# Four small edits to a planned whole-model kernel: the table load asked for first, x's sums on GpSimd, forget columns beside the values, the last bank in two halves

## The chip, the core and the metric

One core of one Trainium2 chip. The metric is the device time of one execution in microseconds; lower is better. TensorE (PE) multiplies, ScalarE (ACT) and VectorE (DVE) do the elementwise work and empty PSUM, GpSimd (POOL) helps, SyncE (SP) issues the transfers.

## The reference, cut to what matters

The kernel computes two two-layer blocks one after the other for 256 tokens of width 1024, in fp32. The change touches the first layer (its norm, values and forget gate), and the end (last MLP and final norm).

```python
# first layer, first block
h = rmsnorm(x, norm_gain[layer])            # x * rsqrt(mean(x*x) + EPS) * gain
proj = h @ w_in_ab[j]                       # 1024 -> 4104 columns
qa, ka, va, ga, qb, kb_, vb_, gb, fb = split_cols(proj, AB_SIZES)   # eight of 512, fb of 8
...                                         # moba attention of qa, ka, va; gate ga
log_f = jax.nn.log_sigmoid(fb + b_forget[j])          # used by fox attention of qb, kb_, vb_
yb = from_heads(fox_attention(qb, kb_, vb_, log_f))
...
# end of the second block
h = h + sq_relu_mlp(rmsnorm(h, norm_mlp[i]), mlp_w_in[i], mlp_w_out[i])
return rmsnorm(h, norm_final)
```

## The kernel before

`describe` (L1651) records every operation as an `Op` with its reads and writes. `Plan.schedule` (L264) then runs a list scheduler with a cost for each instruction (`make`, L497) and a priority (longest path to the end, plus a `boost`), decides for operations given with `nc.either` which engine runs them, and writes one order for each engine. `emit` (L453) issues the instructions in that order, so every engine works strictly in the planned order and waits where an input is late. Line 558 issues nearly all instructions, so the profile's rows are told apart by engine, operation and shape, not by line. Since the order is computed from the whole list, an edit to one operation gives a new order everywhere. `PREFER` (L588) makes the planner avoid GpSimd in every choice that has another engine.

Products are made in fp32r from two rounded parts: `split` (L667) gives `hi` (a rounding copy, ScalarE or VectorE) and `lo = raw - hi` (a subtraction of two SBUF tiles, VectorE), and three matmuls add h*wh, h*wl, l*wh in one bank. Weights come in transfers of 512 KB (1024 columns by 128 partitions), cut by `wtiles` (L671) into pieces of up to 512 columns; each piece is split on ScalarE and VectorE. x arrives in four quarters of 128x2x256; `gained` (L914) multiplies it with the norm's gain and splits it too, in eight chunks. The norm's factor r is not in there: it is put onto the results (`scaled`, `qk_scale`), so the projections don't wait for it.

`setup` (L761) issues the constants, then x's quarters and the first weight pieces in turn on SP's queue. Six matmuls of generated numbers (`WARM`) run first on TensorE. `stats_x` (L909) squares x's quarters, adds them, sums over the partitions with a matmul by ones, and takes the power -0.5 on GpSimd (`rsqrt`). It is recorded with `nc.boost = -2e4`, so the planner ranks it behind nearly all else; its squares run on ScalarE, its adds on VectorE.

`layer_ab` (L1155), for the first mixer: projection of q, then k, then `values` (L1067): 512 columns, for each of 2 token tiles and 8 chunks three matmuls with 512 moving columns into a bank of its own; then `forget` (L1108): a transfer of the 8 forget columns, their split, 24 matmuls with 8 stationary columns and 256 moving ones, two small transposes, then log-sigmoid, cumulative sums by matmul, and GpSimd transfers that spread the result over the partitions. It is read by the second mixer alone.

`mlp(1, True)` (L1508) adds the output projection into four banks, `acc[2 * hf + t]`; in the last of 8 groups a boost orders them one after the other. `finish` (L1574) takes each bank as it is ready: sum with the residual, square with an accumulated sum, product with the gain, and after both halves of a token tile the power, the scaling and two transfers out.

Of the kernel before, what the change touches and what calls it, by code (L numbers as in the profile page):

```python
# [14 lines left out]
AF = mybir.ActivationFunctionType  # L15
OP = mybir.AluOpType
# [132 lines left out]
class Op:  # L149
# [4 lines left out]

AHEAD = 4000.0

LAT = {("T", "A"): 196, ("T", "V"): 196, ("T", "G"): 196, ("A", "T"): 271, ("V", "T"): 256, ("G", "T"): 203,
       ("A", "A"): 143, ("V", "V"): 127, ("G", "G"): 102, ("A", "V"): 142, ("V", "A"): 128, ("A", "G"): 170,
       ("G", "A"): 80, ("V", "G"): 155, ("G", "V"): 80}
# [8 lines left out]
class Plan:  # L168
# [95 lines left out]
    def schedule(self):  # L264
        ops = self.ops
        for o in reversed(ops):
            d = min(f[0] for f in o.forms.values())
            e = next(iter(o.forms))
            best = 0.0
            for s, raw in o.succ.items():  # L270
                e2 = next(iter(s.forms))
                best = max(best, s.cp + (lat(e, e2) if raw or e != e2 else 0))
            o.cp = d + best + (2000 if o.kind == "dma_start" else 0)
        for o in ops:
            o.cp += o.boost
        pools = list(self.pools.values())
        for p in pools:
            p.use = np.zeros(len(ops) + 1, int)
# [13 lines left out]
        table = None  # L292
# [28 lines left out]
        n = 0  # L321
        while n < len(ops):
            best = None
            for e in free:
                f, av = fut[e], avail[e]
                while f and (f[0][0] <= free[e] or ops[f[0][2]].done):
                    r, c, i = heapq.heappop(f)
# [4 lines left out]
                t = free[e] if av else (max(free[e], f[0][0]) if f else None)  # L332
# [5 lines left out]
            t, e = best  # L338
# [15 lines left out]
            o = ops[i]  # L354
# [40 lines left out]
            if o.kind == "dma_start":  # L395
                issue = 480 if e == "S" else 1000
                st = max(t + issue, dma_free)
                dma_free = st + d
                free[e] = t + issue
                o.start, o.end = t, st + d + 3000  # L400
            else:
                o.start, o.end = t, t + d
                free[e] = t + d
# [3 lines left out]
            f0 = front  # L407
            while front < len(ops) and ops[front].done:
                front += 1
            woken = set()  # L410
            for b in o.bufs:
                b.left -= 1
                b.free_at = max(b.free_at, o.end + 150)
                if b.left == 0:
                    tg = self.tags[b.tag]
                    p = tg["pool"]
                    p.free.append((b.free_at, b.slot))
                    tg["used"] -= 1
                    p.use[f0:b.last + 1] -= 1
                    woken.add(p)  # L420
            for p in (pools if front > f0 else woken):
                if waiting[p]:
                    wake(p, t)
# [139 lines left out]
S = 256  # L563
# [49 lines left out]

def rows(k0, n, c0, nc_):

    return lambda w: w[k0 * 128:(k0 + n) * 128, c0:c0 + nc_].reshape(n, 128, nc_).transpose(1, 0, 2)


class Net:
# [141 lines left out]
    def setup(self):  # L761
# [115 lines left out]

        return [self.nc.tile([128, 2, 256], "x", "x") for _ in range(4)]

    def stats_sum(self, x):  # L880

        nc = self.nc
        acc = None
        for v in x:
            k = v.shape[1]
            sq = self.t2([128, k, 256], "ssq")
            nc.either(("G", "tensor_tensor", (sq, v, v), {"op": OP.mult}), ("A", "activation", (sq, v, AF.Square), {}))
            if acc is None:
                acc = sq
            else:  # L890
                nc.either(("G", "tensor_tensor", (acc[:, :k], acc[:, :k], sq), {"op": OP.add}),
                          ("V", "tensor_tensor", (acc[:, :k], acc[:, :k], sq), {"op": OP.add}))
        nc.either(("G", "tensor_tensor", (acc[:, 0], acc[:, 0], acc[:, 1]), {"op": OP.add}),
                  ("V", "tensor_tensor", (acc[:, 0], acc[:, 0], acc[:, 1]), {"op": OP.add}))
# [5 lines left out]
    def rms(self, x):  # L900

        nc = self.nc
        v = self.sm([128, NT], "vv")
        nc.vector.tensor_scalar(v, self.stats_sum(x), 1.0 / D, EPS, op0=OP.mult, op1=OP.add)
        r = self.sm([128, NT], "rstd")
        self.rsqrt(r, v)
        return r

    def stats_x(self):  # L909
        self.rstd = self.rms(self.x)  # L910
# [194 lines left out]
        nc.tensor.matmul(o[:, 128:256], v[1][:, sl], pt[:, 256:384], start=False, stop=True, skip_group_check=True)  # L1105


    def forget(self, w, xt):  # L1108

        nc = self.nc  # L1110
        raw = self.t2([128, NC8, 8], "rawf")
        nc.sync.dma_start(raw.rearrange("p c n -> p (c n)"), w.take(64, rows(0, NC8, 4096, 8)))
        fh = nc.tile([128, NC8, 8], "kr", "fh")
        fl = nc.tile([128, NC8, 8], "kr", "fl")
        self.split(raw, fh, fl)
        f = self.sm([128, NT, 8], "f")
        p8 = self.ps("T")[0:8, 0:256]
        for i in range(NC8):
            self.mm_feat(p8, i == 0, xt, fh[:, i], fl[:, i], i, i == NC8 - 1)
        f8 = self.t2([8, 256], "f8")  # L1120
        self.copy(f8, p8)
        pf = self.ps("T")
        for t in range(NT):
            ps = pf[:, t * 8:(t + 1) * 8]
            nc.tensor.transpose(ps, f8[:, t * 128:(t + 1) * 128], self.ident[:8, :8])
        for t in range(NT):
            ps = pf[:, t * 8:(t + 1) * 8]
            nc.vector.scalar_tensor_tensor(f[:, t], ps, self.rstd[:, t:t + 1], self.bfor, op0=OP.mult, op1=OP.add)
# [26 lines left out]
    def layer_ab(self):  # L1155
# [352 lines left out]
    def mlp(self, l, final=False):  # L1508
# [27 lines left out]
        for g in range(G):  # L1536
            hn = hidden(g + 1) if g + 1 < G else None
            if final:
                pieces = [(hf, p) for hf in range(2) for p in self.wtiles(wout, 4 * g, 4, hf * 512, 512)]
                pieces = [(t, *p) for p in pieces for t in range(NT)]  # L1540
                for t, hf, (wh, wl, k, n) in pieces:
                    nc.boost = 0.0 if g < G - 1 else 6e3 - 1.5e3 * (2 * hf + t)
                    self.mm_tok(acc[2 * hf + t], h, wh, wl, n, k - 4 * g, t, k == 0, k + n == FF // 128)
                nc.boost = 0.0
                h = hn
                continue
            for hf in range(2):
# [9 lines left out]
                            self.add_x(acc[bank], bank, rb2)  # L1557
            h = hn
        if final:
            self.finish(xf, acc)  # L1560

    def x_tok(self):

# [7 lines left out]
                self.copy(xf[t][hf], p)  # L1571
        return xf

    def finish(self, xf, acc):  # L1574
# [5 lines left out]
        ss = self.sm([128, NT, 2], "fss")  # L1580
        v = self.sm([128, NT], "fv")
        y = {}
        nc.gate = None
        for hf in range(2):
            for t in range(NT):
                nc.vector.scalar_tensor_tensor(xf[t][hf], acc[2 * hf + t], self.rstd2[:, t:t + 1], xf[t][hf],
                                               op0=OP.mult, op1=OP.add)
                sq = self.t2([128, 512], "fsq")
                nc.scalar.activation(sq, xf[t][hf], AF.Square, accum_out=ss[:, t, hf:hf + 1])
                y[t, hf] = self.t2([128, 512], "fy")  # L1590
                nc.either(*[(e, "tensor_tensor", (y[t, hf], xf[t][hf], gfin[hf]), {"op": OP.mult}) for e in "VG"])
                nc.vector.tensor_scalar(v[:, t:t + 1], ss[:, t, hf:hf + 1], 1.0 / D, EPS if hf == 0 else v[:, t:t + 1],
                                        op0=OP.mult, op1=OP.add)
        for t in range(NT):
            r = self.sm([128, 1], "fr")
            self.rsqrt(r, v[:, t:t + 1])
            for hf in range(2):
                s = slice(hf * 512, (hf + 1) * 512)
                self.scaled(y[t, hf], y[t, hf], r)
                nc.sync.dma_start(self.out[0, t * 128:(t + 1) * 128, s], y[t, hf])  # L1600

    def stick(self):
        nc, a, xt = self.nc, self.a, self.xt
# [135 lines left out]
```

## Time and profile before

| | |
|---|---|
| median of 3 executions | 954.5 us (953.99 to 956.21) |
| the profiled execution | 955.43 us, its span 953.7 us |
| TensorE busy | 937.4 us, 98% |
| VectorE, ScalarE, GpSimd busy | 671.0, 576.7, 56.0 us |
| granted TensorE clock, mean | 0.997 |

The span runs from the first to the last instruction of the profiled execution; the execution's own time is 1.7 us more. A busy TensorE is one with a matmul under way; matmuls overlap, so how fast they follow one another is read from counts in a stretch.

### The profile page before, as it was taken

What the parts mean: (1) busy time and instruction counts of PE and PEld (TensorE: products, weight loads), DVE (VectorE), ACT (ScalarE), POOL (GpSimd) and SP (SyncE); (2) the same over time, 40 slices, a digit from 0 to 9 for tenths busy, and PEclk for the clock granted to TensorE, in tenths of its full rate; (3) what the DMA queues carried; (4) which work ended last, traced back from release to release, by engine and by line L of the source; (5) the groups of instructions that cost most, each with busy time, mean ns of one, the idle gap of its engine ahead of it and who ended that gap; (6) DMA issues with size and microseconds to landing.
All of it is one profiled execution on the core that took longest, in us unless ns stands there. A gap on an engine that the chain in (4) does not pass through costs nothing.

```text
span 953.7 us, 18145 instructions
## 1 busy us (share of the span) xinstructions
PE 937.4 (98%) x6818; PEld 870.0 (91%) x6818; DVE 671.0 (70%) x1544; ACT 576.7 (60%) x1322; POOL 56.0 (6%) x96
## 2 busy tenths in 40 slices
PE   8999999999999999999999999999999999999997
PEld 6787889889989999999999999999899999899985
DVE  7989887686978765995645556856859865555554
ACT  6877666495676684775555545535756755554453
POOL 1061000310301000000000000000000000000000
PEclk9999999999999999999999999999999999999999
DMA  8654436554434443545566566455626465555541
GB/s 289 216 189 156 121 115 190 166 166 140 142 126 132 145 133 125 164 160 177 171 199 182 177 198 200 153 180 177 180 68 218 131 202 178 177 182 194 194 138 44
DMA packets 45369, 157.13 MB, mean 165 GB/s; under 512 B 5464, under 2 KB 5600, under 8 KB 45280
## 3 DMA queue, kind: packets, MB, share of 16 engines
q1 hardware_dynamic: 44928, 154.91, 50.6%
q0 software_dynamic: 352, 1.06, 0.4%
q8 instruction: 53, 0.87, 0.4%
q14 instruction: 36, 0.29, 0.1%
HBM read 154.89 MB, written 1.06 MB: 164 GB/s over the span
## 4 chain that ended last, share of the span: by engine, by line
PE 91%; DVE 4%; ACT 1%; DMA 1%; issue 1%; POOL 1%; POOLq 0%; SPq 0%; DVEq 0%; ACTq 0%
PE psum L558 91%; DVE r L558 2%; DVE k L558 2%; DMA k<-in_w_in_ab_dram 1%; ACT r L558 1%; ACT k L558 1%; POOL k L558 0%; DMA k<-in_x_dram 0%; ACT L558 0%; POOL cd L558 0%; POOLq L1733 0%; SPq L558 0%; DVEq L558 0%; POOLq L558 0%; ACTq L558 0%
## 5 line engine op out<-in xcount | busy, mean ns | idle before, releaser
L558 PE MATMUL psum<-r,r 128*128 128x256 f32 (+1 forms) x6018 | 878.5, 304 | 5.0 <-ACT r L558 2.7
L558 PEld LDWEIGHTS psum<-r,r 128*128 128x128 f32 x6018 | 792.9, 189 | 55.2 <-issue 6.2
L558 DVE TENSOR_TENSOR r<-k,r 128x512 fp32r<-128x512 f32 (+2 forms) x677 | 410.0, 648 | 138.9 <-ACT r L558 67.6
L558 ACT ACTIVATE r<-k 128x512 fp32r<-128x512 f32 (+2 forms) x606 | 327.3, 591 | 149.1 <-PE psum L558 104.8
L558 ACT ACTIVATE k<-psum 128x256 f32<-128x256 f32 (+4 forms) x166 | 69.1, 449 | 144.5 <-PE psum L558 143.0
L558 PE MATMUL psum<-k,k 128*128 128x128 f32 (+8 forms) x748 | 126.1, 304 | 3.5 <-DVE k L558 2.4
L558 PEld LDWEIGHTS psum<-k,k 128*128 128x128 f32 (+3 forms) x748 | 89.0, 166 | 17.7 <-DVE k L558 3.8
L558 POOL TENSOR_TENSOR k<-k,k 128x2 f32<-128x2 f32 (+3 forms) x42 | 48.3, 1163 | 871.1 <-DVE k L558 870.6
L558 ACT ACTIVATE k<-k 128x256 f32<-128x256 f32 (+5 forms) x151 | 72.6, 505 | 16.5 <-DVE k L558 14.3
L558 ACT ACTIVATE k<-k,k 128x256 f32<-128x256 f32 (+2 forms) x144 | 60.7, 446 | 15.4 <-DVE k L558 13.5
L558 DVE TENSOR_TENSOR k<-k 128x256 f32<-128x256 f32 (+3 forms) x36 | 12.5, 352 | 54.3 <-ACT k L558 54.3
L558 DVE TENSOR_TENSOR k<-psum,k 128x512 f32<-128x512 f32 (+2 forms) x61 | 36.8, 608 | 14.4 <-PE psum L558 13.9
L558 DVE TENSOR_TENSOR k<-k,k 128x512 f32<-128x512 f32 (+5 forms) x92 | 44.2, 492 | 1.2 <-POOL k L558 0.9
L558 ACT ACTIVATE r<-k,k 128x256 fp32r<-128x256 f32 x72 | 33.4, 500 | 18.7 <-DVE k L558 17.5
L558 DVE CAST r<-k 128x512 fp32r<-128x512 f32 (+2 forms) x71 | 27.8, 395 | 14.2 <-ACT k L558 9.5
L558 DVE SCALAR_TENSOR_TENSOR r<-k,k,r 128x256 fp32r<-128x256 f32 x80 | 36.0, 478 | 1.0 <-ACT r L558 0.5
L558 DVE TENSOR_TENSOR r<-psum,r 128x256 fp32r<-128x256 f32 (+1 forms) x36 | 17.8, 508 | 13.8 <-ACT r L558 12.7
L558 DVE TENSOR_SCALAR k<-k,k 128x128 f32<-128x128 f32 (+6 forms) x94 | 22.9, 272 | 6.1 <-POOL k L558 5.5
L558 ACT ACTIVATE r<-psum 128x256 fp32r<-128x256 f32 (+1 forms) x34 | 15.2, 460 | 17.6 <-PE psum L558 15.2
L558 DVE CUSTOM_DVE_ANT_0 k<-psum,k 128x256 f32<-128x256 f32 (+1 forms) x48 | 15.6, 350 | 0.5 <-PE psum L558 0.5
L558 DVE TENSOR_REDUCE k<-k 128x8 f32<-128x512 f32 (+2 forms) x21 | 11.4, 571 | 5.3 <-ACT k L558 5.2
L558 ACT ACTIVATION_READ_ACCUMULATOR k<-k,k 128x1 f32 x80 | 15.1, 189 | 0.0
(42 smaller groups left out, 159.6 us busy)
## 6 DMA issues: line engine op xcount, KB each, us to landing
k<-in_mlp_w_in_dram SPq DMA_DIRECT2D x64, 512.0 KB, 4.2
k<-in_mlp_w_out_dram SPq DMA_DIRECT2D x64, 512.0 KB, 4.5
k<-in_w_in_ab_dram SPq DMA_DIRECT2D x32, 512.0 KB, 4.7
k<-in_w_in_cd_dram SPq DMA_DIRECT2D x26, 512.0 KB, 4.0
k<-in_sb_w_qkv_dram SPq DMA_DIRECT2D x24, 512.0 KB, 4.3
k<-in_xa_w_kv_dram SPq DMA_DIRECT2D x16, 512.0 KB, 4.6
k<-in_w_out_ab_dram SPq DMA_DIRECT2D x8, 512.0 KB, 3.7
k<-in_w_out_cd_dram SPq DMA_DIRECT2D x8, 512.0 KB, 3.7
```

The lines of the kernel that those rows point to most:

```text
L558: return getattr(eng, method)(*[real(a) for a in args], **{k: real(v) for k, v in kw.items()})
```

## The change

Four edits, and three that only name things (`LANDING`, `SHAKE`, and `woken`, which keeps its order).

1. `emit` asks for the first activation table that the planned order needs before it issues anything.
2. `stats_x` gets `"G"`: squares and adds of x's statistics have GpSimd as the only engine, and the boost of -2e4 is gone. Other statistics keep the choice.
3. `forget`'s own projection is gone. `values_forget` projects the first mixer's values in two halves: 256 columns for both token tiles into one bank, then 256 columns and the 8 forget columns together, 264 moving columns, into a bank for each token tile.
4. In the last group of the last MLP the bank of the second token tile and second half is summed as 256 columns into its own bank and then 256 into another (`rest`); `finish` adds and squares the halves separately.

```diff
     def emit(self):
-        table = None
+        table = next(o.table[0] for o in self.order if o.eng == "A" and o.table)
+        self.nc.scalar.preload_act_table_set(table)
...
         self.xt = self.gained(self.x, 0)
-        nc.boost = -2e4
-        self.stats_x()
-        nc.boost = 0.0
+        self.stats_x("G")
...
-    def stats_sum(self, x):
+    def stats_sum(self, x, on="GAV"):
...
-            nc.either(("G", "tensor_tensor", (sq, v, v), {"op": OP.mult}), ("A", "activation", (sq, v, AF.Square), {}))
+            calls = (("G", "tensor_tensor", (sq, v, v), {"op": OP.mult}), ("A", "activation", (sq, v, AF.Square), {}))
+            nc.either(*[c for c in calls if c[0] in on])
...
+                nc.either(*[(e, "tensor_tensor", (acc[:, :k], acc[:, :k], sq), {"op": OP.add}) for e in "GV" if e in on])
+        nc.either(*[(e, "tensor_tensor", (acc[:, 0], acc[:, 0], acc[:, 1]), {"op": OP.add}) for e in "GV" if e in on])
...
-    def forget(self, w, xt):
+    def values_forget(self, w, xt):
+        pa = self.acc()
+        for wh, wl, k, n in self.wtiles(w, 0, NC8, 1024, 256):
+            for t in range(NT):
+                s = slice(t * 128, (t + 1) * 128)
+                o = pa[:, t * 256:(t + 1) * 256]
+                for i in range(k, k + n):
...
+        pb = self.proj_tok(w, xt, [*range(1280, 1536), *range(4096, 4104)], 264)
+        v = []
+        for t in range(NT):
+            v.append(self.t2([128, 512], "v"))
+            self.scaled(v[t][:, 0:256], pa[:, t * 256:(t + 1) * 256], self.rstd[:, t:t + 1])
+            self.scaled(v[t][:, 256:512], pb[t][:, 0:256], self.rstd[:, t:t + 1])
+        return v, *self.forget([p[:, 256:264] for p in pb])
+
+    def forget(self, pf):
...
-        for i in range(NC8):
-            self.mm_feat(p8, i == 0, xt, fh[:, i], fl[:, i], i, i == NC8 - 1)
...
-            v = self.values(w, xt, base + 1024)
             if mix == 0:
-                nc.gate = self.late = nc.seen
-                c, ncb = self.forget(w, xt)
-                nc.gate = None
+                self.late = nc.seen
+                v, c, ncb = self.values_forget(w, xt)
+            else:
+                v = self.values(w, xt, base + 1024)
...
+                if g == G - 1:
+                    for wh, wl, k, n, c in end:
+                        nc.boost = 1.0e3 if c == 0 else 0.0
+                        self.mm_tok((rest if c else acc[3])[:, 0:256], h, wh, wl, n, k - 4 * g, 1, c > 0 and k == 4 * g,
+                                    k + n == FF // 128)
...
+                add(t, hf, whole, acc[2 * hf + t])
+                norm(t, hf, hf, low if (t, hf) == (1, 1) else whole)
+        add(1, 1, high, rest[:, 0:256])
+        norm(1, 1, 2, high)
```

## Rows read from the trace of the kernel before

**Rows 1.** The page's first part: busy us (share of the span) and instructions.

```profile
PE 937.4 (98%) x6818; PEld 870.0 (91%) x6818; DVE 671.0 (70%) x1544; ACT 576.7 (60%) x1322; POOL 56.0 (6%) x96
```

**Rows 2.** TensorE's waits over the span: us in total, times, longest us.

```profile
PE psum L558 <- DVE k L558: 2.4, 4, 1.0
PE psum L558 <- DVE r L558: 2.2, 4, 0.9
```

**Rows 3.** Timeline of the start: start us, us, instructions, idle before and its releaser.

```profile
5.34 1.28 ACT L558 ACT_TABLE_LOAD   x1 [5.34 <-DMA k<-in_x_dram]
...
7.97 1.13 ACT L558 ACTIVATE r<-k 128x512 fp32r<-128x512 f32 x2
...
8.63 19.97 PE L558 MATMUL psum<-r,r 128*128 128x512 f32 x80 [2.70 <-ACT r L558]
```

**Rows 4.** TensorE by stretch: length, busy (matmuls), granted clock, DMA share, GB/s.

```profile
10.00:12.00 2.00, 2.00 (x6) 0.54 1.03 414
12.05:28.40 16.35, 16.35 (x73) 1.00 0.92 320
```

**Rows 5.** TensorE's groups, 8.5 to 12.05 us: busy us, mean ns, idle before.

```profile
L558 PE MATMUL psum<-r,r 128*128 128x512 f32 x8 | 3.6, 622 | 2.7 <-ACT r L558 2.7
```

**Rows 6.** DMA issues at 1.65, 2.12 and 2.59 us: size, us to landing.

```profile
k<-in_w_in_ab_dram SPq DMA_DIRECT2D x1, 512.0 KB, 4.9
k<-in_x_dram SPq DMA_DIRECT2D x1, 256.0 KB, 6.4
k<-in_w_in_ab_dram SPq DMA_DIRECT2D x1, 512.0 KB, 7.2
```

**Rows 7.** VectorE's groups by shape, 7.1 to 19.9 us.

```profile
L558 DVE TENSOR_TENSOR r<-k,r 128x512 fp32r<-128x512 f32 x11 | 7.1, 685 | 0.6 <-ACT r L558 0.6
```

**Rows 8.** Timeline of VectorE, 7 to 19 us.

```profile
7.18 0.88 DVE L558 SCALAR_TENSOR_TENSOR r<-k,k,r 128x256 fp32r<-128x256 f32 x2 [0.53 <-ACT r L558]
...
16.41 0.68 DVE L558 TENSOR_TENSOR r<-k,r 128x512 fp32r<-128x512 f32 x1
...
17.62 1.29 DVE L558 TENSOR_TENSOR r<-k,r 128x512 fp32r<-128x512 f32 x2
```

**Rows 9.** VectorE's groups by shape, 251.7 to 255.7 us.

```profile
L558 DVE TENSOR_TENSOR r<-k,r 128x512 fp32r<-128x512 f32 x2 | 2.5, 1232 | 0.0
L558 DVE TENSOR_TENSOR r<-k,r 128x256 fp32r<-128x256 f32 x1 | 1.0, 979 | 0.0
```

**Rows 10.** VectorE's groups by shape, 241.9 to 251 us.

```profile
L558 DVE TENSOR_TENSOR r<-k,r 128x512 fp32r<-128x512 f32 x7 | 4.6, 683 | 0.0
...
L558 DVE TENSOR_TENSOR r<-k,r 128x256 fp32r<-128x256 f32 x2 | 0.8, 418 | 0.0
```

**Rows 11.** GpSimd's adds by shape, 251.6 to 255.7 us, then 256 to 258 us.

```profile
L558 POOL TENSOR_TENSOR k<-k,k 128x256 f32<-128x256 f32 x4 | 3.5, 902 | 0.4 <-PE psum L558 0.4
...
L558 POOL TENSOR_TENSOR k<-k,k 128x256 f32<-128x256 f32 x2 | 1.4, 736 | 0.5 <-DVE k L558 0.5
```

**Rows 12.** Timeline of GpSimd: its first power.

```profile
52.26 1.95 POOL L558 TENSOR_TENSOR k<-k,k 128x2 f32<-128x2 f32 x2 [46.84 <-DVE k L558]
```

**Rows 13.** TensorE's waits, 60 to 110 us.

```profile
PE psum L558 <- DVE k L558: 1.5, 2, 1.0
```

**Rows 14.** Timeline of TensorE among the forget matmuls (128*8).

```profile
30.18 0.40 PE L558 MATMUL psum<-r,kr 128*8 128x256 f32 x2
30.41 0.39 PE L558 MATMUL psum<-r,r 128*128 128x512 f32 x1
30.64 0.39 PE L558 MATMUL psum<-r,kr 128*8 128x256 f32 x2
```

**Rows 15.** TensorE in a stretch of 256-column matmuls.

```profile
420.00:500.00 80.00, 80.00 (x677) 1.00 0.57 181
```

**Rows 16.** Timeline of the tail, VectorE and ScalarE.

```profile
947.11 0.75 DVE L558 SCALAR_TENSOR_TENSOR k<-psum,k,k 128x512 f32<-128x512 f32 x1
947.90 0.63 ACT L558 ACTIVATE k<-k 128x512 f32<-128x512 f32 x1 [0.60 <-DVE k L558]
...
949.53 0.72 ACT L558 ACTIVATE k<-k,k 128x512 f32<-128x512 f32 x1 [0.92 <-POOL k L558]
```

More of the change, by code (lines that the diff above doesn't have):

```diff
@@ L273, in schedule @@
             o.cp = d + best + (2000 if o.kind == "dma_start" else 0)
+        shake = SHAKE * np.random.default_rng(SEED).standard_normal(len(ops))
         for o in ops:
-            o.cp += o.boost
+            o.cp += o.boost + shake[o.i]
         pools = list(self.pools.values())
@@ L399, in schedule @@
                 free[e] = t + issue
-                o.start, o.end = t, st + d + 3000
+                o.start, o.end = t, st + d + LANDING
             else:
@@ L409, in schedule @@
                 front += 1
-            woken = set()
+            woken = {}
             for b in o.bufs:
@@ L419, in schedule @@
                     p.use[f0:b.last + 1] -= 1
-                    woken.add(p)
+                    woken[p] = 0
             for p in (pools if front > f0 else woken):
@@ L1105, in pv_feat @@
         nc.tensor.matmul(o[:, 128:256], v[1][:, sl], pt[:, 256:384], start=False, stop=True, skip_group_check=True)
-    def forget(self, w, xt):
+    def values_forget(self, w, xt):
         nc = self.nc
[L1111 to L1115, printed above, removed]
-        f = self.sm([128, NT, 8], "f")
-        p8 = self.ps("T")[0:8, 0:256]
-        for i in range(NC8):
-            self.mm_feat(p8, i == 0, xt, fh[:, i], fl[:, i], i, i == NC8 - 1)
-        f8 = self.t2([8, 256], "f8")
-        self.copy(f8, p8)
-        pf = self.ps("T")
-        for t in range(NT):
[L1124 to L1128, printed above, removed]
+        pa = self.acc()
[4 more added lines that the diff above has]
+                for i in range(k, k + n):
+                    f = dict(stop=False, skip_group_check=True)
+                    nc.tensor.matmul(o, xt[0][i][:, s], wh[:, i - k], start=i == 0 and t == 0, **f)
+                    nc.tensor.matmul(o, xt[0][i][:, s], wl[:, i - k], start=False, **f)
+                    f["stop"] = i == NC8 - 1
+                    nc.tensor.matmul(o, xt[1][i][:, s], wh[:, i - k], start=False, **f)
+        pb = self.proj_tok(w, xt, [*range(1280, 1536), *range(4096, 4104)], 264)
[5 more added lines that the diff above has]
+        return v, *self.forget([p[:, 256:264] for p in pb])
@@ L1129, in forget @@
+    def forget(self, pf):
+        nc = self.nc
+        f = self.sm([128, NT, 8], "f")
+        for t in range(NT):
+            nc.vector.scalar_tensor_tensor(f[:, t], pf[t], self.rstd[:, t:t + 1], self.bfor, op0=OP.mult, op1=OP.add)
         ab = self.sm([128, NT, 8], "fab")
@@ L1540, in mlp @@
                 pieces = [(t, *p) for p in pieces for t in range(NT)]
+                if g == G - 1:
+                    rest = self.ps("S")
+                    end = [(wh[:, :, c:c + 256], wl[:, :, c:c + 256], k, n, c) for c in (0, 256)
+                           for t, hf, (wh, wl, k, n) in pieces if (t, hf) == (1, 1)]
+                    pieces = [p for p in pieces if p[:2] != (1, 1)]
                 for t, hf, (wh, wl, k, n) in pieces:
@@ L1559, in mlp @@
         if final:
-            self.finish(xf, acc)
+            self.finish(xf, acc, rest)
     def x_tok(self):
@@ L1572, in x_tok, with finish @@
         return xf
-    def finish(self, xf, acc):
+    def finish(self, xf, acc, rest):
         nc = self.nc
@@ L1579, in finish, with add, norm @@
         gfin = [self.bc("gfin", "t2", g[hf], 512) for hf in range(2)]
-        ss = self.sm([128, NT, 2], "fss")
+        nc.gate = None
+        ss = self.sm([128, NT, 3], "fss")
         v = self.sm([128, NT], "fv")
-        y = {}
-        nc.gate = None
+        y = [[self.t2([128, 512], "fy") for _ in range(2)] for _ in range(NT)]
+        def add(t, hf, sl, ps):
+            x = xf[t][hf][:, sl]
+            nc.vector.scalar_tensor_tensor(x, ps, self.rstd2[:, t:t + 1], x, op0=OP.mult, op1=OP.add)
+        def norm(t, hf, c, sl):
+            x = xf[t][hf][:, sl]
+            sq = self.t2([128, 512], "fsq")
+            nc.scalar.activation(sq[:, sl], x, AF.Square, accum_out=ss[:, t, c:c + 1])
+            nc.either(*[(e, "tensor_tensor", (y[t][hf][:, sl], x, gfin[hf][:, sl]), {"op": OP.mult}) for e in "VG"])
+            nc.vector.tensor_scalar(v[:, t:t + 1], ss[:, t, c:c + 1], 1.0 / D, EPS if c == 0 else v[:, t:t + 1],
+                                    op0=OP.mult, op1=OP.add)
+        whole, low, high = slice(0, 512), slice(0, 256), slice(256, 512)
         for hf in range(2):
             for t in range(NT):
[L1586 to L1593, printed above, removed]
+                add(t, hf, whole, acc[2 * hf + t])
+                norm(t, hf, hf, low if (t, hf) == (1, 1) else whole)
+        add(1, 1, high, rest[:, 0:256])
+        norm(1, 1, 2, high)
         for t in range(NT):
```

23 lines of the change are left out of this document (12 added, 11 removed).

## The prediction

> **What bounds the kernel now.** I read the page's engine rows first. TensorE is busy for 937.4 of 953.7 us [rows 1], so the kernel is TensorE work in a row, and only two things can change the time: the work on that engine and its idle time. The view of TensorE's waits comes next: VectorE is waited for eight times, 4.6 us in all [rows 2]. The timeline of the start shows a longer wait, 2.7 us, for ScalarE: its table load begins at 5.34, when the first quarter of x has landed, the first weight piece is rounded at 7.97, and the first real matmul follows at 8.63 [rows 3]. The windows then show a granted clock of 0.54 between 10 and 12 us, behind that gap, mostly the lower of its two levels, 1.2 instead of 2.4 GHz, and 1.00 from 12.05 on [rows 4]. Eight matmuls start from 8.63 to 12.05 [rows 5], 0.427 us each; from 12.05 on, 73 of 512 columns start within 16.35 us, 72 steps of 0.227 [rows 4]. The first projection (48 matmuls) therefore ends at 12.05 + 40 x 0.227 = 21.1 us. The reader is to see that in this first stage TensorE is fed by pairs of instructions on ScalarE and VectorE, and that VectorE works there almost without a pause.
>
> **The table asked for ahead.** The load's 1.28 us leave the path that starts TensorE, unless another stands behind it. The first weight piece is issued at 1.65 and lands 4.9 us later, at 6.55 [rows 6], and its rounding (0.61) would end at 7.25 instead of 8.58. Taken alone: TensorE starts 1.33 us sooner. Its idle gap would then be 1.4 us instead of 2.7; if the clock stayed up, the second weight piece, landing at 2.59 + 7.2 = 9.8 [rows 6], would set the pace: rounded at 10.45, then 36 matmuls, end 18.6, a gain of 2.5. So this stage's lower end is -2.5 us, and -1.3 if the slow stretch only moves. The second load, at 25, delays nothing that TensorE waits for; it counts as nothing.
>
> **x's sums on GpSimd.** Four squarings leave ScalarE, and three adds of 128x512 and a fold leave VectorE, about 0.60 each where they follow one another (0.685 with the overlap [rows 7]; a pair takes 1.29 [rows 8]). GpSimd gets eight two-input instructions in a row: four squarings and three adds of 512 columns, one fold of 256. The trace of before has no 512-wide one. The nearest rows are the 128x256 adds near 252 us: while four of them run, VectorE's two-input instructions take 1.232 us for 512 columns and 0.979 for 256 [rows 9], against 0.683 and 0.418 just before [rows 10]. VectorE is held 0.55 us by each, one of its instructions per GpSimd instruction; GpSimd is held too, 0.902 against 0.736 when VectorE has none of that kind [rows 11]. Doubled for 512 columns (an estimate; the ends are 0.55, if the hold doesn't grow, and 1.47, twice the whole 0.736) that is 1.1 us.
>
> The Trainium skill, "SBUF — State Buffer", section "SBUF: two separate sides", says that a two-input VectorE instruction and a GpSimd instruction exclude each other on a shared port pair for a whole instruction. The rows agree that they exclude each other, but show 0.55 of 0.736 us; by the Trainium skill's rule the sum below would be 2.4 us longer.
>
> The place is the worst one: every piece that TensorE multiplies in this stage needs a 128x256 subtraction of x and a 128x512 one of the weights on VectorE, both two-input [rows 7, 8]. The first squaring (from 5.4 us) falls partly into VectorE's pause of 0.53 before 7.18 [rows 8], and the rest of it is made up by the earlier first rounding. The other seven instructions start when the second quarter of x lands, 2.12 + 6.4 = 8.5 [rows 6], and run back to back with VectorE's: 6 x 1.1 + 0.55 = 7.2 us of holding. Before, the last weight subtraction of the first projection ends at 17.1 [rows 8], behind two of the adds; now at 17.1 - 1.2 + 7.2 = 23.1. The holds end near 19.4, with the fifth of eight pieces due at about 20.4; VectorE then makes a piece in 1.0 us and TensorE needs 6 x 0.227 = 1.36, so TensorE sets the end: 20.4 + 22 x 0.227 = 25.4, against 21.1. I take +4.3 us for the stage, in which the table's gain is lost. Ends: -2.5 (holds that cost nothing) and +6.7 (1.47 each). TensorE starves from about 10 to 20 us, so a half clock there costs little; behind it, it does (a rival).
>
> **What the sums give back.** Before, the statistics were ranked last: GpSimd's first power is at 52.26, after 46.84 us idle [rows 12]. All scaling of q, k and v waits for it, and VectorE then works through it; TensorE waits 1.5 us for it between 60 and 110 us [rows 13]. With the sums done near 20, r is ready some 30 us sooner and this work spreads out; TensorE, itself later, waits less too. Of the 1.5 I take -1.2; ends -1.5 and +1.0, since the planner orders the whole kernel anew and may open a wait of the size of those there are [rows 2]. Late behind it come the weight transfers that wait for VectorE to free their buffers: they slip by up to 6 us, but TensorE reaches those pieces over 5 us later as well, so I add nothing.
>
> **Forget columns in the values.** Removed: 24 matmuls with 8 weight columns. Two of them and one of 512 columns repeat every 0.46 us [rows 14], so each takes (0.46 - 0.227) / 2 = 0.117: 2.8 us; two small transposes, some 0.1 each by the pace of 256 columns. Changed: 48 matmuls of 512 columns become 48 of 256 and 48 of 264. In a stretch of 256-column ones 677, two of them tiny, take 80.0 us, 0.1185 each [rows 15]; 8 columns more are 0.004. So 48 x (0.1185 + 0.1225 - 0.227) = 0.7 us are added. Sum: -3.0 + 0.7 = -2.3 us. TensorE runs without a pause there, so it counts in full; if the 512-column pace is 0.231, it is -2.5, and if weight preparation (eight pieces of 264 columns in place of four of 512) held it up, -1.5. One small DMA and its rounding go, and there is one more accumulator bank for a while. The log-sigmoid chain moves behind the values; its result is needed only by the second mixer, one projection and four pairs of heads later.
>
> **Last bank in two halves.** Before, the tail is: sum 0.75, squaring 0.63 plus the reading of its accumulator, two small steps, the power, scaling 0.72 from 949.53, and the transfer [rows 16]. Now the last sum and square are of 256 columns. By the pair 0.683 and 0.418 [rows 10] the sum saves 0.27; the square saves between nothing and half, I take 0.2; 24 matmuls of 0.1185 in place of 12 of 0.227 add 0.12. Sum -0.35; ends -0.5 and +0.1, the latter if the first half's small steps stand in VectorE's queue ahead of the last sum. Scaling and transfers stay whole. The named landing time (3000 as before), the shake of 0 and the ordered set change nothing.
>
> **Sum.** +4.3 - 1.2 - 2.3 - 0.35 = +0.45 us on the profiled execution's 955.4 us, of which 1.7 lie outside its span. That execution stands 0.9 above the median of 954.5, so against the median I forecast **954.9 us: no change that a measurement can tell** (0.2%, 1.9 us, is about that bound).
>
> **Rivals.** *Faster, 949.5.* The holds hide: VectorE or the transfers had slack there, and the first projection ends between 18.6 and 19.8 us. Then -1.9 - 0.5 - 2.3 - 0.35 = -5.0. For it speaks that before, the last subtraction was done 2.9 us before TensorE needed it; against it, that 7.2 us are more than that. It decides if the holds add less than about 3 us to VectorE's last piece. A milder form, holds of 0.55 each (3.9 instead of 7.2), gives 951.6.
> *Slower, 957.2.* VectorE is held for the whole 0.736 per 256 columns, 1.47 for 512: 6 x 1.47 + 0.74 = 9.6 instead of 7.2, +2.4. This is the rule of the Trainium skill named above. It decides from about 1.35 us per hold. Against it speaks the 0.55 worked out above [rows 9, 10].
> *Slower, 956.5.* The starved stretch lowers the clock as the 2.7 us gap did, and the projection's last eight matmuls run at the slow pace of 0.427: +1.6. One such stretch stands behind a shorter gap [rows 3, 4].
> *The change isn't what it says:* if a load still stood before ScalarE's first copy, 1.28 us would return, but in my main case VectorE covers it; the time stays.
>
> **Chances.** No change 0.40, the faster case with its milder form 0.33, the two slower ones 0.15 and 0.12. So faster 0.33, same 0.40, slower 0.27. The range takes in most of the faster case and both slower ones: 949.5 to 958.0; the main case alone has 954.2 with the low ends of its three small terms together, and 957.1 with the largest high one.
>
> **What would show it.** The table load would stand before 2 us. Behind 8.5 us GpSimd's 512-wide instructions would alternate with VectorE's, whose 512-column subtractions would take about 1.8 us instead of 0.685; TensorE would pause from about 10 us, and its first 48 matmuls would end near 25.4. If they end before 20, the holds were the wrong step. The first power would be at about 20 us, TensorE's wait for VectorE in 60 to 110 us mostly gone, no matmul with 8 weight columns left, and from the last matmul to the end 0.4 us less. I am wrong above all if VectorE keeps its pace under GpSimd's sums, or if the new order opens a wait of more than 2 us later on.

## The result, and the profile after

The changed kernel is slower: 961.7 us median of 6 executions (960.7 to 962.9) against 955.4 of 6 (954.0 to 956.2) of the kernel before; ratio 1.0070, 95% interval 1.0057 to 1.0083. That is above the range that was given (949.5 to 958.0). Its profiled execution has a span of 960.0 us against 953.7, so 6.3 us are to be found.

The page's first part, of the changed kernel:

```profile
PE 940.2 (98%) x6852; PEld 876.4 (91%) x6852; DVE 675.6 (70%) x1546; ACT 583.4 (61%) x1328; POOL 67.3 (7%) x104
```

TensorE's work hardly changed [rows 1]; its waits did (us, times, longest; the view of [rows 2]):

```profile
PE psum L564 <- DVE k L564: 5.7, 4, 2.3
PE psum L564 <- DVE r L564: 3.5, 2, 2.6
```

**The start.** Timeline of the changed kernel, ScalarE, then GpSimd, VectorE and TensorE:

```profile
0.73 1.28 ACT L460 ACT_TABLE_LOAD   x1 [0.73 <-PEq L1753]
...
5.47 1.14 POOL L564 TENSOR_TENSOR k<-k 128x512 f32<-128x512 f32 x1
8.08 3.49 POOL L564 TENSOR_TENSOR k<-k 128x512 f32<-128x512 f32 x2 [1.48 <-DMA k<-in_x_dram]
11.54 1.47 POOL L564 TENSOR_TENSOR k<-k,k 128x512 f32<-128x512 f32 x1
12.96 1.23 POOL L564 TENSOR_TENSOR k<-k 128x512 f32<-128x512 f32 x1
14.14 3.14 POOL L564 TENSOR_TENSOR k<-k,k 128x512 f32<-128x512 f32 x2
17.36 1.06 POOL L564 TENSOR_TENSOR k<-k 128x256 f32<-128x256 f32 x1
...
9.42 5.04 DVE L564 SCALAR_TENSOR_TENSOR r<-k,k,r 128x256 fp32r<-128x256 f32 x4
14.38 3.45 DVE L564 TENSOR_TENSOR r<-k,r 128x512 fp32r<-128x512 f32 x2
17.76 1.34 DVE L564 SCALAR_TENSOR_TENSOR r<-k,k,r 128x256 fp32r<-128x256 f32 x2
...
8.94 4.61 PE L564 MATMUL psum<-r,r 128*128 128x512 f32 x12 [0.81 <-DVE r L564]
16.20 15.04 PE L564 MATMUL psum<-r,r 128*128 128x512 f32 x58 [2.65 <-DVE r L564]
```

The load stands at 0.73 instead of 5.34 [rows 3]. From 8 us on GpSimd's 512-column instructions run back to back with VectorE's: two subtractions that took 1.29 [rows 8] take 3.45, 1.08 us more for each of the two GpSimd instructions beside them; two of 256 columns that took 0.88 take 1.34 beside the fold. TensorE starves at 13.5 and gets its next piece at 16.20. The windows (length, busy, granted clock, DMA share, GB/s; as [rows 4]) show what this does to the clock and to the transfers:

```profile
10.00:12.00 2.00, 2.00 (x6) 0.50 1.03 420
12.00:14.00 2.00, 1.55 (x5) 0.71 1.03 420
14.00:16.00 2.00, 0.00 (x0) 1.00 0.20 80
16.00:18.00 2.00, 1.80 (x5) 0.65 0.00 0
18.00:20.00 2.00, 2.00 (x6) 0.50 0.52 115
20.00:31.00 11.00, 11.00 (x50) 1.00 0.86 301
```

The granted clock is 0.50, wholly the lower level, already between 10 and 12 us, behind waits of 0.80 and 0.81 us at 7.40 and 8.94, and again from 18 to 20 us, behind the long pause. The transfers stop for some 3 us, since VectorE has freed no buffer: between 8 and 20 us SyncE's queue waits for it twice, 10.7 us in all. The 48th matmul of the first projection starts at 25.41, against 20.89 in the trace of before. A second loss stands behind it, in TensorE's timeline: the column sums of x (one moving column), two matmuls, and then a wait for VectorE, which itself waits for GpSimd's power (0.72 us from 31.86):

```profile
31.08 0.50 PE L564 MATMUL psum<-k,k 128*128 128x1 f32 x4
31.44 0.70 PE L564 MATMUL psum<-r,r 128*128 128x512 f32 x2
33.02 0.49 PE L564 MATMUL psum<-k,k 128*128 128x128 f32 x2 [0.88 <-DVE k L564]
33.62 11.72 PE L564 MATMUL psum<-r,r 128*128 128x512 f32 x50
```

At 0.227 each the two matmuls take TensorE to 31.9, the two of 128x128 columns need some 0.2, and the next stands at 33.62: some 1.5 us are lost, an estimate, 0.88 of them in the wait that the profile shows. In e3, described below, twelve matmuls stand there in place of two, and no wait opens.

**Where the rest went.** The column sums of the next norm are landmarks: they end the first layer, and then the second. In the timeline of before they stand here:

```profile
178.34 0.50 PE L558 MATMUL psum<-k,k 128*128 128x1 f32 x4
...
295.54 0.28 PE L558 MATMUL psum<-k,k 128*128 128x1 f32 x2
```

and in the changed kernel here (the line between them is the column sums of the cross-attention's memory, `mem_setup`, which before stood at 49 us, beside x's):

```profile
180.53 0.50 PE L564 MATMUL psum<-k,k 128*128 128x1 f32 x4
...
245.23 0.28 PE L564 MATMUL psum<-k,k 128*128 128x1 f32 x2
...
302.25 0.28 PE L564 MATMUL psum<-k,k 128*128 128x1 f32 x2
```

So: +4.5 us at the 48th matmul, +1.5 at 32 us, back to +2.2 at the end of the first layer (-3.8 on the way), +6.7 at the end of the second (+4.5 in it), +6.3 at the end. The 4.5 us are at the four pairs of sliding-window heads, `layer_cd`'s last part. The timeline of the changed kernel there, TensorE, VectorE, GpSimd:

```profile
264.23 0.93 PE L564 MATMUL psum<-k,k 64*128 64x128 f32 x8 [0.69 <-ACT k L564]
267.49 1.91 PE L564 MATMUL psum<-k,k 64*128 64x128 f32 x8 [2.33 <-DVE k L564]
...
262.00 4.36 DVE L564 TENSOR_TENSOR r<-k,r 128x512 fp32r<-128x512 f32 x5
266.28 0.47 DVE L564 CUSTOM_DVE_ANT_0 k<-psum,k,k 128x256 f32<-128x256 f32 x1
...
260.86 0.40 POOL L564 COPY k<-k 128x256 f32<-128x256 f32 x1
262.20 0.73 POOL L564 COPY k<-k 128x256 f32<-128x256 f32 x1 [0.95 <-DVE k L564]
263.58 2.23 POOL L564 TENSOR_TENSOR k<-k,k 128x256 f32<-128x256 f32 x2 [0.64 <-PE psum L564]
```

The heads' scores stand in their banks at 265, the softmax (CUSTOM) waits on VectorE behind five weight subtractions, two of which GpSimd's adds hold, and TensorE has nothing else to do until the softmax is done. In the kernel before, 45 matmuls of the next projection stand behind the same scores and cover that time:

```profile
255.50 5.57 PE L558 MATMUL psum<-r,r 128*128 128x256 f32 x45
```

Between 225 and 290 us TensorE's waits sum to 4.7 us here and to 1.2 before. Behind the longest one the granted clock falls too: 0.58 from 265 to 270 us and 0.74 from 270 to 275, where it was 1.00 before. So the layer's 4.5 us are more than the 3.5 us of waits.

**The tail**, timeline of the changed kernel, VectorE and ScalarE (answers to [rows 16]): the last sum and square are of 256 columns, 0.48 and 0.42 in place of 0.75 and 0.63.

```profile
953.97 0.48 DVE L564 SCALAR_TENSOR_TENSOR k<-psum,k,k 128x256 f32<-128x256 f32 x1
...
954.49 0.42 ACT L564 ACTIVATE k<-k 128x256 f32<-128x256 f32 x1 [0.34 <-DVE k L564]
```

From the start of the last matmul to the end are 6.4 us instead of 7.0.

### The profile page after: what moved, and what is told of

Its sections match the earlier page's. It is cut to its first block, busy times and chain, and to the rows that moved or that the text cites. A ratio compares the mean times of both kernels' runs of the same rounds, so it can differ in the third digit from the quotient of the medians.

```text
span 960.0 us, 18196 instructions
## 1 busy us (share of the span) xinstructions
PE 940.2 (98%) x6852; PEld 876.4 (91%) x6852; DVE 675.6 (70%) x1546; ACT 583.4 (61%) x1328; POOL 67.3 (7%) x104
## 4 chain that ended last, share of the span: by engine, by line
PE 92%; DVE 3%; DMA 2%; issue 1%; ACT 1%; POOL 0%; SPq 0%; POOLq 0%; DVEq 0%; ACTq 0%
PE psum L564 92%; DVE k L564 2%; DVE r L564 2%; DMA k<-in_w_in_ab_dram 2%; ACT k L564 0%; POOL k L564 0%; SPq L564 0%; ACT r L564 0%; POOLq L1765 0%; DVEq L564 0%; ACTq L564 0%; POOLq L564 0%
## 5 line engine op out<-in xcount | busy, mean ns | idle before, releaser
L564 PE MATMUL psum<-r,r 128*128 128x256 f32 (+2 forms) x6078 | 882.8, 303 | 4.8 <-DVE r L564 3.5
L564 DVE TENSOR_TENSOR r<-k,r 128x512 fp32r<-128x512 f32 (+3 forms) x681 | 411.7, 646 | 158.1 <-PE psum L564 75.1
L564 ACT ACTIVATE r<-k 128x512 fp32r<-128x512 f32 (+3 forms) x607 | 328.7, 593 | 153.1 <-PE psum L564 103.5
L564 ACT ACTIVATE k<-psum 128x256 f32<-128x256 f32 (+5 forms) x165 | 68.3, 451 | 145.4 <-PE psum L564 142.4
L564 PE MATMUL psum<-k,k 128*128 128x128 f32 (+6 forms) x746 | 127.6, 307 | 7.7 <-DVE k L564 5.7
L564 POOL TENSOR_TENSOR k<-k,k 128x2 f32<-128x2 f32 (+4 forms) x45 | 52.2, 1170 | 880.2 <-DVE k L564 647.1
L564 PEld LDWEIGHTS psum<-k,k 128*128 128x128 f32 (+2 forms) x746 | 88.8, 169 | 21.5 <-DVE k L564 8.4
L564 ACT ACTIVATE k<-k,k 128x256 f32<-128x256 f32 (+3 forms) x139 | 59.0, 449 | 10.0 <-DVE k L564 8.0
L564 DVE TENSOR_SCALAR k<-k,k 128x128 f32<-128x128 f32 (+7 forms) x100 | 24.8, 273 | 7.5 <-POOL k L564 4.3
L564 DVE SCALAR_TENSOR_TENSOR k<-psum,k 128x256 f32<-128x256 f32 (+2 forms) x24 | 12.1, 505 | 4.5 <-PE psum L564 2.5
```

The costliest lines, as they stand in the source:

```text
L564: return getattr(eng, method)(*[real(a) for a in args], **{k: real(v) for k, v in kw.items()})
```

## The experiments

Medians; the kernel before, timed beside each group of runs, had 954.9 to 955.1. The last column is TensorE's waits between 225 and 290 us, summed from the view of waits.

| kernel | us | ratio to before, 95% interval | waits |
|---|---|---|---|
| before | 955.1 | | 1.2 |
| changed (edits 1 to 4) | 961.7 | 1.0070 (1.0057 to 1.0083) | 4.7 |
| e1: edit 1 | 952.5 | 0.9972 (0.9962 to 0.9981) | 1.2 |
| e2: edit 1, x's sums moved, order of before | 958.0 | 1.0034 (1.0021 to 1.0047) | 1.2 |
| e3: edits 1, 3, 4 | 952.6 | 0.9979 (0.9970 to 0.9988) | 4.7 |
| e4: changed, memsets for the sums | 959.3 | 1.0048 (1.0034 to 1.0061) | 4.6 |
| e5: edits 1, 3 | 951.7 | 0.9966 (0.9954 to 0.9979) | 4.7 |
| e6: edits 1, 4 | 952.1 | 0.9968 (0.9956 to 0.9981) | 1.2 |
| e7: changed, sums left out | 954.5 | 0.9995 (0.9986 to 1.0004) | 4.7 |
| e8: e3 shaken, seed 1 | 955.5 | 1.0002 (0.9993 to 1.0011) | 4.6 |
| e9: e3 without window adds | 951.2 | 0.9958 (0.9946 to 0.9971) | 4.2 |
| e10: e3, window adds on VectorE | 960.2 | 1.0059 (1.0045 to 1.0073) | 5.9 |
| e11: e1 shaken | 953.4 | 0.9987 (0.9978 to 0.9995) | 1.0 |
| e12: e3 shaken, seed 2 | 959.6 | 1.0047 (1.0035 to 1.0060) | 6.4 |
| e13: e3, memory statistics first | 948.6 | 0.9940 (0.9928 to 0.9953) | 1.2 |
| e14: e1, memory statistics last | 959.6 | 1.0051 (1.0038 to 1.0064) | 7.1 |
| e15: changed, memory statistics first | 956.8 | 1.0026 (1.0015 to 1.0038) | 0.4 |
| e16: e12, memory statistics first | 953.1 | 0.9979 (0.9970 to 0.9988) | 2.0 |

### The start: is it GpSimd's work?

**e1**, the table load alone, in the kernel before:

```diff
-        table = None
+        table = next(o.table[0] for o in self.order if o.eng == "A" and o.table)
+        self.nc.scalar.preload_act_table_set(table)
```

> The kernel before with the table asked for ahead of all and nothing else: every engine's order is unchanged. If the table load was what held the first matmul, TensorE starts near 7.3 us instead of 8.63 and the whole is 1.3 us faster (954.1 against 955.4), 2.5 us (952.9) if the clock then stays up. If the pace of VectorE or of the transfers hides it, no change (955.4).

It gains 2.6 us. TensorE's first two real matmuls start at 7.12 instead of 8.63, the others run from 8.10 without a pause, and the granted clock from 10 to 12 us is 1.00 instead of 0.54:

```profile
8.10 14.15 PE L559 MATMUL psum<-r,r 128*128 128x512 f32 x61 [0.25 <-DVE r L559]
```

**e2**, the same, and x's eight sums issued on GpSimd at the places that the plan of before gave them:

```diff
-            o.forms[o.eng][1]()
+            o.forms["G" if o in self.moved else o.eng][1]()
```

> As e1, but x's four squares, three adds and fold are issued on GpSimd, at the places that the plan of before gave them; all other orders stay. If GpSimd's sums hold VectorE (theory 1), the first projection ends 4 to 6 us later than in e1 and the whole is 3 to 6 us slower than e1, with VectorE's 512-column subtractions at 1.7 us or more between 8 and 19 us. If the loss of the changed kernel comes from its new order (theory 2), it is no slower than e1, since ScalarE and VectorE have eight instructions less.

It loses 5.5 us on e1 with the same order everywhere else: two weight subtractions took 3.20 us here, 1.28 in e1, and the granted clock was 0.50 from 10 to 16 us.

```profile
8.99 3.20 DVE L559 TENSOR_TENSOR r<-k,r 128x512 fp32r<-128x512 f32 x2
```

**e4**, the changed kernel's order with memsets in the place of the sums (`o.go` replaces the instruction when it is issued):

```diff
+                o.go = lambda out=out: nc.nc.gpsimd.memset(out.real(), 1.0)
```

> The changed kernel with every engine's order unchanged, but GpSimd fills the tiles of x's squares and sums with a constant in place of reading x: the statistic of x isn't computed. Theory 1: nothing holds VectorE, the first projection ends before 20 us, the start gives back about 6 us and the whole is near 955.5, with the waits between 260 and 280 us still there. Theory 2: near 961, since the order is the same.

This was no clean cut: the eight memsets needed no input, ran in a row, and held VectorE in another way. TensorE got its second piece only at 10.36, after a pause of 2.36 us, and the granted clock was 0.50 from 10 to 16 us. So its 959.3 us can't decide between the two theories. A 128x128 TENSOR_SCALAR that takes 0.21 us in e1 took 2.31:

```profile
5.36 3.81 POOL L807 MEMSET k<- 128x512 f32 x8
...
5.96 2.31 DVE L564 TENSOR_SCALAR k<-k 128x128 f32<-128x128 f32 x1
```

**e7** leaves the sums out altogether, but for one 128x256 memset:

```diff
+                o.go = (lambda: None) if nc.moved else lambda out=out[:, 0]: nc.nc.gpsimd.memset(out.real(), 1.0)
```

> The changed kernel, its planned orders kept, with the eight GpSimd instructions of x's sums left out but for one 128x256 memset in the first one's place; x's statistic is not computed. Theory, GpSimd's sums hold VectorE and so make the start long: the start stage ends some 6 us sooner, no half clock before 20 us, 954 to 955.5 us, the wait of about 2.3 us near 262 us still there. Rival, the order that the change gave the start (x's quarters ahead of the weights) is what costs: 959 to 961 us.

954.5: the GpSimd instructions, with the lower clock that followed them, cost 7.2 us of the changed kernel's time, and the order they came in is not at fault for the first projection. VectorE's lines of the changed kernel come back to their old pace (5.04 to 1.66, 3.45 to 1.29), and TensorE's to that of e1; the wait behind x's column sums stays:

```profile
8.57 1.66 DVE L564 SCALAR_TENSOR_TENSOR r<-k,k,r 128x256 fp32r<-128x256 f32 x4
10.26 1.29 DVE L564 TENSOR_TENSOR r<-k,r 128x512 fp32r<-128x512 f32 x2
...
8.11 14.07 PE L564 MATMUL psum<-r,r 128*128 128x512 f32 x60 [0.28 <-DVE r L564]
...
26.23 0.49 PE L564 MATMUL psum<-k,k 128*128 128x128 f32 x2 [0.88 <-DVE k L564]
```

So the order that edit 2 gives costs 954.5 - 952.6 = 1.9 us beside e3, although e7 does none of the work of x's sums and e3 does all of it.

### The second layer: where does its wait come from?

**e3**, the changed kernel with `stats_x` as before:

```diff
-        self.stats_x("G")
+        nc.boost = -2e4
+        self.stats_x()
+        nc.boost = 0.0
```

> The changed kernel with x's sums as before (squares on ScalarE, adds on VectorE, ranked last): the edits to the table, the forget columns and the last bank alone. Theory 1: the start is that of e1 (1.3 to 2.5 gained), forget -2.3, tail -0.4, so 950 to 951.5. Theory 2: a new order costs here as well, waits of TensorE of 8 us or more between 245 and 340 us and a whole of 953 to 956.

952.6, between the two theories and no better than e1: the forget edit's gain is gone, and the wait is there without edit 2. By the landmarks the first layer ends 4.2 us before e1's (171.11 against 175.28) and the second at the same place (292.32 against 292.45). x's column sums stand at 21.6 us here although their rank is the low one again.

```profile
235.88 0.28 PE L564 MATMUL psum<-k,k 128*128 128x1 f32 x2
...
258.20 1.92 PE L564 MATMUL psum<-k,k 64*128 64x128 f32 x8 [2.35 <-DVE k L564]
```

**e5 and e6**, e3 without the code of edit 4, and e3 without that of edit 3 (the kernel before with edits 1 and 3, and with 1 and 4).

> The kernel before with edits 1 and 3 (table load ahead, forget columns in the values). Theory 1, the forget edit's saved work counts in full and the wait of 2.35 us at the heads of the sliding-window layer belongs to the tail edit's order: 952.5 - 2.1 = 950.4 us. Theory 2, the order that comes with the forget edit opens that wait: about 952.6 to 953 us, with a pause of TensorE of over 2 us near 258 us.

> The kernel before with edits 1 and 4 (table load ahead, last bank in two halves). If the tail edit saves its 0.35 to 0.6 us and opens no wait: 951.9 to 952.2 us, and some 45 projection matmuls still fill the heads of the sliding-window layer. If the wait there comes with this edit's new order: about 954.5 to 955 us.

The wait comes with edit 3. e6, which has the three naming edits too, has none and gains 0.45 on e1; e5 gains 0.85, where its work is 2.3 us less. e3 lies 0.9 above e5, though the spans of their profiled executions are both 950.1; that is not settled.

**e8 and e12**, e3 with the planner's ranks shaken by some 100 ns:

```diff
-SHAKE, SEED = 0.0, 0
+SHAKE, SEED = 100.0, 1
```

> The kernel of edits 1, 3 and 4 (x's sums as before) with the priorities of the planner changed at random by some 100 ns (shake 100, seed 1): the same operations in another order. If the wait at the sliding-window heads belongs to one order and not to the edits: about 949.5 to 950.5 us and no pause over 1 us near 260 us. If the edits' work itself brings it: 952.6 us.

> Edits 1, 3 and 4 with the priorities shaken by 100 ns, seed 2. If the wait at the heads goes with the forget edit whatever the order: a pause of about 2.3 us near 255 us again. If it is one order's: no pause over 1.2 us there, and 949.5 to 951 us where no other wait opens.

**e11**, the same with e1, whose forget columns are as before.

> The kernel before with edit 1 and its priorities shaken at random by 100 ns: no edit to the work. If the order of before is a lucky one and any new order costs: 954 to 956 us, as the shaken kernel of edits 1, 3 and 4 lost 2.9 us. If orders near by are as good and that loss comes with the forget edit: 952 to 953 us, with projection matmuls still filling the sliding-window heads.

The wait is not one order's luck: of these orders each with the forget edit has one over 2 us (2.35 in e3, 2.3 in e8 and, in e12, 3.7, there for GpSimd), and the one shaken e1 has none over 0.7. The times fit neither theory: e8 lies above both of its own, e11's 953.4 between its two, and e12's 959.6 far above e3. In e8 the waits sum to as much as in e3, but the granted clock from 255 to 260 and from 260 to 265 us was 0.72 and 0.60, in e3 0.83 in both.

**e9**, e3 in its own order without six of the window adds, and **e10**, e3 with all eight on VectorE:

```diff
-                nc.gpsimd.tensor_tensor(bw, self.bias8[h], self.wmask, op=OP.add)
+                nc.vector.tensor_tensor(bw, self.bias8[h], self.wmask, op=OP.add)
```

> The kernel of edits 1, 3 and 4, its orders kept, without six of the eight GpSimd adds (128x256) that join bias and window mask of the sliding-window heads; their sums are left out of the computation. If those adds hold VectorE and so make the wait at the heads long: VectorE's five subtractions near 253 us take 3.1 instead of 4.37 us, TensorE's wait there falls from 2.35 to about 1.1 us, 951.0 to 951.4 us in place of 952.6. If the wait is the order's alone (five subtractions ahead of the softmax, no projection left to fill): 952.4 to 952.7 us.

> The kernel of edits 1, 3 and 4 with those eight adds on VectorE, 0.42 us each, a complete one that computes what the reference does. If the holding is what counts and the new order is no worse: 951 to 952 us. If a new order alone moves the time by as much: anywhere between 950 and 955 us, with the wait at the heads in another place or gone.

e9: the five subtractions take 3.29 instead of 4.37, the wait falls from 2.35 to 1.27, and the time by 1.4. The holding makes the wait longer, but half of it is there without. All waits together fall by 0.5 us only (4.7 to 4.2); the granted clock from 255 to 265 us, 1.00 against 0.83 in e3, has a part in the rest. e10 missed its range, at 960.2: the new order has a wait of 4.2 us for ScalarE at the same place.

```profile
259.03 1.80 PE L564 MATMUL psum<-k,k 128*128 128x128 f32 x6 [4.23 <-ACT k L564]
```

What all orders with the wait share is the place of the memory's statistics. In e3, e5, e8, e9, e10 and e12 their column sums stand at 235 to 238 us, just ahead of the heads; in e1, e6 and e11 at 47 to 50. In the changed kernel GpSimd then copies the window's keys only at 260.9 and 262.2 (243.1 and 251.4 before), and the scores come late for the projections that could have covered the softmax. GpSimd's own queue is not what makes these copies late: ahead of the power -0.5 of the keys' norm it sat idle for 6.23 us, waiting for VectorE.

```profile
258.65 1.08 POOL L564 TENSOR_TENSOR k<-k,k 128x2 f32<-128x2 f32 x1 [6.23 <-DVE k L564]
```

So the keys themselves come late in the new order; how the planner gets from late statistics to late keys is not shown. The next four runs edit only the rank of these statistics, and the planner orders the rest anew.

**e13**, e3 with them ranked first (e15 and e16 likewise, in the changed kernel and in e12), and **e14**, e1 with them ranked last (-1e4):

```diff
+    n.nc.boost = 2e5
     n.mem_setup()
+    n.nc.boost = 0.0
```

> Edits 1, 3 and 4 with one more: the statistics of the cross-attention's memory (mem_setup) ranked first, so that they come at the start of the first layer and not just ahead of the sliding-window heads. Theory, their place is what opens the wait of 2.35 us there: it goes, projection matmuls fill the heads again, and forget's 2.1 us and the tail's 0.45 count: 952.5 - 2.5 = 950.0, taken as 949.7 to 950.7 us. Rival, the lost matmuls of the forget columns were filler and their absence is what opens it: 952.4 to 953 us.

> The kernel before with edit 1, its memory statistics ranked last, so that they fall ahead of the sliding-window heads as in the changed kernel; the forget columns as before. Theory as for the run before: a pause of over 2 us opens at the heads, 955 to 957 us. Rival, the forget edit is needed for it: 952 to 953 us and no pause over 1.2 us there.

> The changed kernel, all four edits, with the memory statistics ranked first. Theory: only the second loss goes, 961.7 - 2.5 = 959.2 us, taken as 958.5 to 959.7; the start stays as long as in the changed kernel. Rival: 961.5 us, or the start's length changes too.

> Edits 1, 3 and 4 shaken by 100 ns with seed 2, as in the run of 959.6 us, and the memory statistics ranked first. Theory: the pause of 3.9 us at the heads goes in this order too: 953 to 956 us (its start stage stays some 4 us long). Rival, the shaking itself made the pause: 959 to 960 us.

e13, TensorE and GpSimd: the sums at 52.64, the window's keys copied at 234.85 and 243.12, and 45 projection matmuls cover the softmax.

```profile
52.64 0.50 PE L564 MATMUL psum<-k,k 128*128 128x1 f32 x4
...
247.24 5.63 PE L564 MATMUL psum<-r,r 128*128 128x256 f32 x45
...
234.85 0.40 POOL L564 COPY k<-k 128x256 f32<-128x256 f32 x1 [13.41 <-DVE r L564]
...
243.12 0.40 POOL L564 COPY k<-k 128x256 f32<-128x256 f32 x1 [3.25 <-PE psum L564]
```

The first rival falls: the forget matmuls were not needed as filler. e13, e15 and e16 gain 4.0, 4.9 and 6.5 us on e3, the changed kernel and e12, more than the wait alone and, in e13 and e15, more than was expected; in e13 the granted clock from 245 to 285 us is back at 1.00. e14 loses 7.1 us on e1 without the forget edit, more than expected; there it is seven waits for VectorE, 6.4 us in all and the longest 1.4, two of them ahead of the heads, rather than one over 2 us at them. So what a late place costs depends on the rest of the order.

```profile
242.31 0.50 PE L559 MATMUL psum<-k,k 128*128 128x1 f32 x4
244.07 0.79 PE L559 MATMUL psum<-k,k 128*128 128x128 f32 x2 [1.26 <-DVE k L559]
246.28 1.26 PE L559 MATMUL psum<-k,k 128*128 128x128 f32 x5 [1.41 <-DVE k L559]
```

The landmarks tell the same for all kernels. From the end of the first layer to that of the second it is 115.3 to 117.2 us in the eight with the memory's statistics early (the kernel before, e1, e2, e6, e11, e13, e15, e16), and 121.1 to 125.3 in nine with them late (the changed kernel, e3 to e5, e7, e8, e10, e12, e14); e9, with six adds left out, has 119.2. The two groups don't overlap, with or without the forget edit.

e13 computes what the reference does and is faster than both kernels: 948.6 us, 0.6% under the kernel before.

## Why the prediction was wrong

- **The step that failed** is what the sum allowed for the new order. It stands in the term "What the sums give back": "ends -1.5 and +1.0, since the planner orders the whole kernel anew and may open a wait of the size of those there are [rows 2]", and of this term -1.2 was taken, so in the sum the new order costs nothing. It cost some 6 us. It opened a wait of 0.9 us with its small gaps at 32 us (+1.5; e7 has that wait without the sums' work) and, far off, the one at the sliding-window heads (+4.5 in that layer; e13 and e15 take it away). [Rows 2] gave waits that the order before had left, and these are no bound for what another order leaves: a wait there was kept short by 45 filler matmuls that the term did not look at. The text's last sentence named this as a way to be wrong; no rival had it.
- **The sum against the landmarks.** Start +4.5 (forecast +4.3), new order +1.5 and +4.5 (0), the rest of the first layer -3.8 (forget and give-back together -3.5), the tail -0.4 (-0.35). Together +6.3 us, where the forecast had +0.45.
- **Start stage, +4.3.** Right in mechanism and nearly in size (4.5). The holds are 1.08 us for 512 columns (1.1 taken) and 0.46 for 256 (0.55), TensorE pauses from 13.5 instead of about 10, GpSimd's first power is at 31.86 instead of about 20, and the 48th matmul starts at 25.41, where the end was put at 25.4. Against e1, the kernel that keeps edit 1's gain, whose 48th matmul starts at 18.46, the stage costs 7.0 us, and the whole kernel gets 7.2 back in e7.
- **The clock.** The rival of 956.5 was right that a half clock follows; it stands in the starved stretch and until 20 us, and not at the last eight matmuls, since the clock is 1.00 from 20 us on. The stage still ended near the 25.4 of the main case, but no run of the changed kernel separates what the clock cost. That it can cost is seen in e4: x's column sums stand 4.7 us later than in e7 (28.97 against 24.29), more than the one pause of 2.36 us, with the clock at 0.50 from 10 to 16 us. At the heads, which the prediction did not look at, it fell as well.
- **The whole-instruction rival, 957.2.** Its price of 1.47 was a doubled 0.736, but GpSimd's single 512-column instructions took 1.14 to 1.47 with VectorE busy beside them, and 1.10 at the least in e2. So 1.08 lies just below the shortest whole instruction seen. The Trainium skill, "SBUF — State Buffer", section "SBUF: two separate sides", gives the hold as a whole instruction: at 512 columns the trace agrees within 0.1 us of the shortest ones, at 256 it shows 0.46 to 0.55, less than the 0.74 of [rows 11].
- **The table's lower end, -2.5**, taken alone: measured -2.6 (e1).
- **What the sums give back, -1.2.** Not shown: between 60 and 110 us TensorE still waits 1.5 us for VectorE [rows 13]. The wait is gone in e15, which has x's sums at the same place, so this too hangs on the order. r is ready early, but edit 2 was not needed for it: in e3, without edit 2, the column sums stand at 21.6 us too.
- **Forget, -2.3.** The work went (the first layer ends 3.8 us sooner than its start stage allows in the changed kernel), but the saving as a whole was 0.85 us in e5, since this edit's order moves the memory's statistics. With those back in the first layer, edits 3 and 4 give 3.9 us (e1 to e13), and less the tail's 0.45 that is some 3.4 for forget, more than the 2.3; what made it more is not shown.
- **Tail, -0.35.** Measured -0.45 (e6), -0.6 from the last matmul to the end.

Why the planner puts the memory's statistics behind the first layer once the forget columns are in the values stays open.

## What to carry to other kernels

When one plan orders the whole kernel, cost an edit in two runs: its instructions in the old order (e2), and the new order without its instructions (e7); here they were +5.5 on e1 and +1.9 on e3. A long matmul run that hides a softmax is cover, and a new order can take it away far from the edit: after each edit compare the time from landmark to landmark, and try pinning side work early, as e13 does. Don't put two-input work on GpSimd while VectorE's two-input work sets the pace, even where GpSimd is idle 94% of the time.

## What the runs showed of the hardware

GpSimd's memsets held VectorE too, but other instructions: in e4, beside eight memsets of 128x512 from 5.36 to 9.17 us, a one-input TENSOR_SCALAR of 128x128 stood for 2.31 us (0.21 in e1) and a CAST for 0.55 (0.21), while the two-input instructions that ran with the first of them, until 6.04, kept their pace (four in 1.42 us, as in e1), and so did two from 8.84 beside the last one (0.86 us; 0.87 in e1). The section of the Trainium skill named above says that a VectorE instruction in a mode that uses two ports contends with any GpSimd instruction, and a two-input one only with a GpSimd instruction that reads SBUF. The rows agree with both halves, if the TENSOR_SCALAR ran in such a mode, which no run here shows by itself.
